# Fewer score groups, an earlier weight load and a narrower spread in a decoder layer

## The chip, the core and the metric

The kernel runs on one core of one Trainium2 chip. TensorE (PE) does the matrix products, VectorE (DVE) and ScalarE (ACT) the elementwise work and the moves out of the accumulators (PSUM), GpSimd (POOL) a few small things, and SyncE (SP) issues nearly all transfers. The metric is the device time of one execution, in microseconds (us).

## The reference

One layer of a decoder trunk, 512 tokens of width 1024, in float32:

```
mod = silu(c) @ w_ada + b_ada            # six rows of 1024: shift, scale, gate, twice
h = rmsnorm(x) * (1 + scale1) + shift1
q,k,v (sliding), q,k,v (differential), two gates = split(h @ w_in)
A: 8 heads of 64, 2 key heads, window 128, ALiBi, a learned sink in the softmax
B: 4 heads, two causal softmax maps each, p0 - lambda * p1, times v; per-head rmsnorm
x += gate1 * ((sigmoid(ga) * (A @ w_a) + sigmoid(gd) * (B @ w_b)) @ w_out)
x += gate2 * convffn(rmsnorm(x) * (1 + scale2) + shift2)
out = rmsnorm(x)
```

## The kernel before

Products are taken at nearly full float32 precision from a faster float type: each operand is split into a high and a low part, and `mm3` (L119 to L121) issues three matmuls, high x high, high x low, low x high. The weights come as float32 into one of four buffers with the tag "raw" (512 KB each); `split` then makes the high half on ACT (a cast, L115) and the low half on DVE (a subtraction, L116). A raw buffer is free once both have read it. All these loads are issued by SP, in one order, and SP waits where the next load's buffer is not yet free.

The work has four stages. To about 60 us: two modulation rows, the first norm, and the first six column blocks of the input projection. From 60 to about 330 us: the attention with the rest of the projection, the gates and the branch products. Then the output projection, the MLP (up L1126, down L1735), and a short tail.

In the attention the order of PE's program is written out by hand (`tc.manual_schedule` for the tensor engine); DVE, ACT, POOL and SP get theirs from the framework's scheduler, which places instructions by its own estimates, by priorities (`tc.high_priority`) and by marks that an instruction comes behind another (`tc.issue_after`). PE's filler is `fill(n)`: n steps, each one `mm3` of 128x512 matmuls of the current projection unit. Units lie in the list `units`; two are loaded ahead. `after(n, fn)` puts a small piece of work behind n further steps, and every eighth step the generator `ada_rows` is advanced by one.

Between filler stand the attention's own pieces:

- Sliding heads, in four pairs (i = 0 to 3). `swa_scores` (L532) computes the scores of two query blocks as a group of small matmuls on the upper and lower 64 rows of the array side by side (`mm3_rows`, L126), into two PSUM banks; a DVE reduction (L559) adds the bias and takes the row maximum. `swa_softmax`: ten exponentials on ACT (L571, L574), then DVE divides (L578 to L582). `swa_transpose` (L593): transposes on PE, copies to `pT` on ACT (L595). `swa_values` (L604): the product with v in two column tiles of 64 columns; `evac` (L430, L431) takes the result out as high part on ACT and low part on DVE (`outal`).
- Differential heads, 16 steps of (head, query block). `diff_scores` (reduction at L673), `diff_softmax` (exponentials L687, scalings L692 and L693 on DVE), `diff_transpose` (L702), and once a head `diff_values` (`od`).

PSUM tags: two banks for filler, three for scores (`sbank`), two for transposes and small spreads (`tbank`), one for the value products (`vbank`).

The other modulation rows are made in the attention by `ada_rows`: for each of four rows and two halves, four loads `ra` of two k-blocks (L750), each followed in the same step by two DVE multiply-adds into `arow` (L755, L757). The 128 partitions of `arow` are then summed: `split` makes `arh` and `arl`, and `ada_spread` multiplies them by a square of ones on PE (L766, L767, tile `pr`), copies one row out on ACT (L769) and sends it to memory on POOL's queue (`mod_rows`, L770).

The order of the sliding pieces in one turn of the loop is:

```
        if more:
            swa_scores(i + 1, 0)
        fill(SWA_FILL[3])
        swa_transpose(i, 0)
        fill(SWA_FILL[4])
        swa_transpose(i, 1)
        if more:
            swa_scores(i + 1, 2)
        fill(SWA_FILL[5])
        ...
        nxt = {0: (), 1: (s + 1,), 2: (s + 1,), 3: (s + 1, s + 2)}[n] if s < 15 else ()
```

The last line is the differential loop's choice of the blocks that are scored in a step.

Of the kernel before, what the change touches and what calls it, by code (L numbers as in the profile page):

```python
# [8 lines left out]
F32 = mybir.dt.float32  # L9
# [44 lines left out]
def kernel(  # L54
# [41 lines left out]
    def sbank(name, shape=(P, S)):  # L96
        return bank("s", 3, list(shape), name)
# [7 lines left out]
    def raw_tile(shape, name):  # L105
        return wp.tile(shape, F32, tag="raw", bufs=4, name=name)
# [26 lines left out]
    warm = cpool.tile([P, 1], F32, name="warm")  # L133
    nc.vector.memset(warm, 0.0)
    nc.scalar.activation(warm, warm, AF.Exp)
    onesr = cpool.tile([P, P], F32R, name="onesr")
    nc.vector.tensor_copy(onesr, ones)
    mhalf = cpool.tile([P, 4], F32, name="mhalf")
    nc.gpsimd.memset(mhalf, -0.5)
    qsc = cpool.tile([P, 4], F32, name="qsc")  # L140
# [388 lines left out]
    class Pair:  # L529
        pass  # L530

    def swa_scores(i, n0):  # L532
        if n0 == 0:
            c = pairs[i] = Pair()
            c.mx, c.nm, c.lsum, c.es = (
                ap.tile([P, 2, NT], F32, tag=t, bufs=2, name=f"{t}{i}") for t in ("mx", "nm", "lsum", "es")
            )
            c.sb = [ap.tile([P, 2, P], F32, tag="st0", bufs=2, name=f"st{i}_0")]
            c.sb += [ap.tile([P, 2, 256], F32, tag="st", bufs=ST, name=f"st{i}_{n}") for n in range(1, NT)]
            c.pT = []  # L540
        c = pairs[i]
        sps = [sbank(f"sw{i}_{n0}_{j}", (P, 2, 256)) for j in range(2)]
        for n in (n0, n0 + 1):
            w = P if n == 0 else 2 * P
            k0 = max(0, n - 1) * P
            qs, ks = slice(n * P, (n + 1) * P), slice(k0, k0 + w)
            mm3_rows([
                (
                    sps[j][:, n - n0, :w],
                    [qa[64 * j : 64 * j + 64, i, b, qs] for b in range(2)],  # L550
                    [ka[64 * j : 64 * j + 64, b, ks] for b in range(2)],
                )
                for j in range(2)
            ])
        for n in (n0, n0 + 1):
            w = P if n == 0 else 2 * P
            for j in range(2):
                with tc.high_priority(offset=HP):
                    c.last = nc.vector.tensor_tensor_reduce(  # L559
                        c.sb[n][:, j, :w], sps[j][:, n - n0, :w], dsw[:, 256 - w : 256], 1.0, -3e38, ALU.add, ALU.max,  # L560
                        c.mx[:, j, n : n + 1],
                    )

# [20 lines left out]
    def swa_transpose(i, j):  # L584
        c = pairs[i]
        pt = ap.tile([P, 1024], F32, tag="aTh" if j == 0 else "aTl", bufs=2, name=f"pT{i}_{j}")
        for b in range(2):
            wb = 512 if b == 0 else 384
            tp = tbank(f"tp{i}_{j}_{b}")
            for m in range(wb // P):  # L590
                kb, n = 2 * b + m // 2, 2 * b + m // 2 + m % 2
                off = (kb - max(0, n - 1)) * P
                nc.tensor.transpose(tp[:, m * P : (m + 1) * P], c.sb[n][:, j, off : off + P], ident)  # L593
            with tc.high_priority(offset=HP):
                nc.scalar.copy(pt[:, b * 512 : b * 512 + wb], tp[:, :wb])  # L595
        c.pT.append(pt)

    def swa_values(i):
        o = vbank(f"oa{i}")
        for kb in (0, 2, 1, 3):  # L600
            w = P if kb == 3 else 2 * P
            for j in range(2):
                rows = slice(64 * j, 64 * j + 64)
                nc.tensor.matmul(  # L604
                    o[rows, kb * P : kb * P + w], va[:, kb, rows],
                    pairs[i].pT[j][:, kb * 256 : kb * 256 + w],
                    start=kb == 0, stop=kb == 3, tile_position=(0, 64 * j),
                )
        evac(outa[0][:, i], outa[1][:, i], o)


    heads = {}
# [35 lines left out]
    def diff_scores(*ss):  # L648
        ops = []
        for s in ss:  # L650
            h, n = divmod(s, NT)
            t = heads[h]
            w = (n + 1) * P
            if n == 0:
                firsts[h] = [sbank(f"sd{h}_{m}", (P, 2, 256)) for m in range(2)]
            sps = [firsts[h][m][:, n, :w] if n < 2 else sbank(f"sd{h}_{n}_{m}")[:, :w] for m in range(2)]
            mm3_rows([
                (
                    sps[m],
                    [t[64 * m : 64 * m + 64, b, n * P : (n + 1) * P] for b in range(2)],  # L660
                    [t[64 * m : 64 * m + 64, 2 + b, :w] for b in range(2)],
                )
                for m in range(2)
            ])
            ops.append((s, sps, w))
        for s, sps, w in ops:
            h, n = divmod(s, NT)
            mx = ap.tile([P, 2], F32, tag="dmx", bufs=3, name=f"dmx{h}_{n}")
            pm = []
            for m in range(2):  # L670
                st = ap.tile([P, w], F32, tag="st", bufs=ST, name=f"sd{h}_{n}_{m}")
                with tc.high_priority(offset=HP):
                    nc.vector.tensor_tensor_reduce(  # L673
                        st, sps[m], ddf[:, 512 - w : 512], 1.0, -3e38, ALU.add, ALU.max, mx[:, m : m + 1]
                    )
                pm.append(st)
            scored[s] = mx, pm
# [62 lines left out]

    mod_rows = tc.dram_tile([4, D], F32, name="mod_rows")

    def ada_rows():
        for idx in range(4):
            for hf in range(2):
                c0 = (2 + idx) * D + hf * S
                ac = big.tile([P, S], F32, tag="sq2", name=f"arow{idx}{hf}")
                for k in range(0, KT, 2):
                    r = raw_tile([P, 2, S], f"ra{idx}{hf}_{k}")
                    nc.sync.dma_start(r, wada[k * P : (k + 2) * P, c0 : c0 + S].rearrange("(a p) n -> p a n", p=P))  # L750
                    with tc.high_priority(offset=HP // 2) if tick[0] > ADA_EASY else ExitStack():
                        for a in range(2):
                            cc = cs[:, k + a : k + a + 1]
                            if k + a == 0:
                                nc.vector.tensor_scalar_mul(ac, r[:, a], cc)  # L755
                            else:
                                nc.vector.scalar_tensor_tensor(ac, r[:, a], cc, ac, ALU.mult, ALU.add)  # L757
                    yield
                ah = big.tile([P, S], F32R, tag="g2b0", name=f"arh{idx}{hf}")
                al = big.tile([P, S], F32R, tag="g2b1", name=f"arl{idx}{hf}")  # L760
                split(ah, al, ac)
                after(ADA_LAG, lambda idx=idx, hf=hf, ac=ac, ah=ah, al=al: ada_spread(idx, hf, ac, ah, al))

    def ada_spread(idx, hf, ac, ah, al):
        pr = tbank(f"pr{idx}{hf}")
        nc.tensor.matmul(pr, onesr, ah, start=True, stop=False)  # L766
        nc.tensor.matmul(pr, onesr, al, start=False, stop=True)  # L767
        row = ac[0:1, :]
        nc.scalar.copy(row, pr[0:1, :])  # L769
        nc.gpsimd.dma_start(mod_rows[idx : idx + 1, hf * S : (hf + 1) * S], row)  # L770


    pair_w = {}
# [29 lines left out]
    add_head(0)  # L803
    add_head(1)
    fill(SWA_FILL[0])
    swa_scores(0, 0)
    with tc.issue_after(pairs[0].last.ins):
        fill(SWA_FILL[1])
        swa_scores(0, 2)
    with tc.issue_after(pairs[0].last.ins):  # L810
        swa_softmax(0)
        fill(1)
# [2 lines left out]
        fill(SWA_FILL[2] - 1)  # L815
    for i in range(SWA_PAIRS):
        more = i + 1 < SWA_PAIRS
        if more:
            swa_scores(i + 1, 0)
        fill(SWA_FILL[3])  # L820
        swa_transpose(i, 0)
        fill(SWA_FILL[4])
        swa_transpose(i, 1)
        if more:
            swa_scores(i + 1, 2)
        fill(SWA_FILL[5])
        if more:
            swa_softmax(i + 1)
        fill(SWA_FILL[6])
        swa_values(i)  # L830
        fill(SWA_FILL[7])
# [11 lines left out]
    for s in range(4 * DIFF_HEADS):  # L843
        h, n = divmod(s, NT)
        if n == 0 and 0 < h < 3:
            add_head(h + 1)
        elif s == 12:
            add_gate_a(2)
            add_gate_a(3)
        fill(DIFF_FILL[1])  # L850
        nxt = {0: (), 1: (s + 1,), 2: (s + 1,), 3: (s + 1, s + 2)}[n] if s < 15 else ()
        if nxt:
            diff_scores(*nxt)
        fill(DIFF_FILL[2])
        diff_transpose(s)
        for z in nxt:
            diff_softmax(z)
        if n == 0 and h:
            diff_values(h - 1)
            fill(DIFF_FILL[3])  # L860
# [926 lines left out]
```

## Time and profile before

| | us |
|---|---|
| runs shown | 706.75, 707.45, 707.52; median 707.45 |
| the profiled execution | 708.24, of which the span from first to last instruction is 705.4 |
| TensorE clock granted, mean | 0.994 |
| ACT busy in the span | 383.9 |
| DVE busy from 120 to 220 us | 83.03 of 100 |
| modulation multiply-adds (L757), 56 of them | 41.9, 747 ns each |
| modulation loads `ra`, 32 of 512 KB | 4.2 median from issue to landing |

A line of the costliest groups names the line of code, the engine, the operation, what it writes and reads (by the program's names, buffer numbers left out), partitions x elements, and the count; then the busy time and the mean of one in ns; then the idle time of the engine just before these instructions with what ended it. The records of filler matmuls overlap, so that one takes 0.39 us although the next starts 0.23 later: what PE can do is read from start to start. Busy times of an engine that is not the one that sets the end cost nothing by themselves.

### The profile page before, as it was taken

How to read it: one execution, taken by the hardware profiler on the slowest of the kernel's cores; microseconds unless marked ns; L12 is line 12 of the kernel's file. 1: busy time of each engine (PE TensorE's matmuls, PEld its weight loads, DVE VectorE, ACT ScalarE, POOL GpSimd, SP SyncE). 2: the span in 40 equal slices, each digit the busy share in tenths (PEclk: the TensorE clock that was granted, in tenths of full speed). 3: DMA queues.
4: the chain of work that ended last, by engine and by line, in shares of the span. 5: the costliest groups of instructions: out<-in, count | busy, mean ns of one | idle time of the engine just before them, and what ended most of it. 6: DMA issues, size and time to landing. Idle time of an engine off the chain costs nothing. (4 is left out here: it accounts for less than half of the span.)

```text
span 705.4 us, 11197 instructions
## 1 busy us (share of the span) xinstructions
PE 685.0 (97%) x4155; PEld 597.1 (85%) x4155; DVE 578.4 (82%) x1107; ACT 383.9 (54%) x676; POOL 82.2 (12%) x100
## 2 busy tenths in 40 slices
PE   6999999999999999999999999999999999999994
PEld 6777777777787888888889999999999999888884
DVE  5998968788985766773579899888888999979996
ACT  3646766545543333431468656555555666656664
POOL 3000000000011000000030111111101102530300
PEclk9999999999999999999999999999999999999998
DMA  9983624263543774529617888786979748996803
GB/s 311 302 262 98 201 61 154 67 199 90 170 153 100 262 214 142 186 93 288 187 33 148 197 199 204 177 209 182 208 204 230 164 143 204 197 200 191 158 0 119
DMA packets 115861, 121.80 MB, mean 173 GB/s; under 512 B 4415, under 2 KB 93280, under 8 KB 115808
## 3 DMA queue, kind: packets, MB, share of 16 engines
q1 hardware_dynamic: 96894, 95.09, 42.7%
q0 software_dynamic: 18720, 25.73, 21.6%
q8 instruction: 32, 0.52, 0.3%
q10 hardware_dynamic: 194, 0.28, 0.1%
q14 instruction: 21, 0.17, 0.1%
HBM read 118.97 MB, written 2.11 MB: 172 GB/s over the span
## 5 line engine op out<-in xcount | busy, mean ns | idle before, releaser
L1126 PE MATMUL up<-t,m_whi 128*128 128x256 f32 x528 | 96.1, 283 | 0.0
L1126 PEld LDWEIGHTS up<-t,m_whi 128*128 128x128 f32 x528 | 82.3, 192 | 0.0
L1126 PE MATMUL up<-t,m_wlo 128*128 128x256 f32 x264 | 74.7, 283 | 0.1
L1126 PE MATMUL up<-bh,p_wlo 128*128 128x256 f32 x232 | 65.7, 284 | 0.7 <-DVE p_wlo L1069 0.7
L1126 PE MATMUL up<-bh,p_whi 128*128 128x256 f32 x232 | 65.6, 283 | 0.0
L1126 PE MATMUL up<-bl,p_whi 128*128 128x256 f32 x232 | 65.6, 283 | 0.0
L1126 PEld LDWEIGHTS up<-t,m_wlo 128*128 128x128 f32 x264 | 50.6, 192 | 0.3 <-DVE m_wlo L1069 0.3
L1126 PEld LDWEIGHTS up<-bh,p_wlo 128*128 128x128 f32 x232 | 44.5, 192 | 1.1 <-DVE p_wlo L1069 1.1
L1126 PEld LDWEIGHTS up<-bh,p_whi 128*128 128x128 f32 x232 | 44.5, 192 | 0.0
L1126 PEld LDWEIGHTS up<-bl,p_whi 128*128 128x128 f32 x232 | 44.5, 192 | 0.0
L757 DVE SCALAR_TENSOR_TENSOR arow<-ra,cs,arow 128x512 f32<-128x512 f32 x56 | 41.9, 747 | 2.6 <-DMA ra<-in_w_ada_dram 1.8
L1037 POOL DMA_DIRECT2D s<-in_w_up_dram x21 | 27.0, 1361 | 142.9 <-DMA s<-in_w_up_dram 78.0
L1069 DVE TENSOR_TENSOR m_wlo<-s,m_whi 128x1024 fp32r<-128x1024 f32 x31 | 37.7, 1217 | 2.0 <-ACT m_whi L1065 2.0
L1065 ACT CAST m_whi<-s 128x1024 fp32r<-128x1024 f32 x31 | 32.5, 1047 | 9.4 <-DVE s L1059 5.9
L1126 PE MATMUL up<-t,p_whi 128*128 128x256 f32 x176 | 32.2, 283 | 0.0
L687 ACT ACTIVATE sd<-sd,dmx 128x128 f32<-128x128 f32 (+3 forms) x32 | 17.8, 556 | 23.2 <-DVE dmx L685 15.9
L175 POOL TENSOR_TENSOR r<-ms,mhalf 128x1 f32<-128x1 f32 (+1 forms) x16 | 13.2, 828 | 144.7 <-DVE ms L173 74.0
L1126 PEld LDWEIGHTS up<-t,p_whi 128*128 128x128 f32 x176 | 27.4, 192 | 0.2 <-issue 0.2
L1133 ACT ACTIVATE gT<-a,cv 128x512 f32<-128x512 f32 x22 | 17.7, 813 | 17.6 <-DVE a L1168 17.3
L770 POOL DMA_DIRECT2D mod_rows<-arow x8 | 4.3, 540 | 193.7 <-ACT arow L769 193.5
L1065 ACT CAST p_whi<-wa 128x1024 fp32r<-128x1024 f32 x18 | 18.7, 1041 | 12.0 <-PE up L1126 7.2
L1126 PE MATMUL up<-t,p_wlo 128*128 128x256 f32 x88 | 24.9, 283 | 0.0
(478 smaller groups left out, 2073.0 us busy)
## 6 DMA issues: line engine op xcount, KB each, us to landing
ra<-in_w_ada_dram SPq DMA_DIRECT2D x32, 512.0 KB, 4.2
wa<-in_w_up_dram SPq DMA_DIRECT2D x22, 512.0 KB, 4.6
s<-in_w_up_dram SPq DMA_DIRECT2D x21, 512.0 KB, 5.1
s<-in_w_up_dram POOLq DMA_DIRECT2D x21, 512.0 KB, 7.0
adaw<-in_w_ada_dram SPq DMA_DIRECT2D x16, 512.0 KB, 4.9
w<-in_w_in_dram SPq DMA_DIRECT2D x12, 512.0 KB, 4.1
a<-in_w_up_dram SPq DMA_DIRECT2D x11, 512.0 KB, 4.8
b<-in_w_down_dram SPq DMA_DIRECT2D x10, 512.0 KB, 4.7
```

Of the source, the lines that this page charges most:

```text
L175: nc.gpsimd.tensor_tensor(r0, ms, mhalf[:, :n], ALU.pow)
L687: nc.scalar.activation(pm[m], pm[m], AF.Exp, bias=mx[:, m : m + 1], scale=slope, accum_out=lsum[:, m : m + 1])
L757: nc.vector.scalar_tensor_tensor(ac, r[:, a], cc, ac, ALU.mult, ALU.add)
L770: nc.gpsimd.dma_start(mod_rows[idx : idx + 1, hf * S : (hf + 1) * S], row)
L1037: nc.gpsimd.dma_start(dst, upblock(*blk), accum_op=ALU.add)
L1065: nc.scalar.copy(W[J, name][0], R[J, SRC[name]])
L1069: nc.vector.tensor_sub(lo, R[J, SRC[name]], hi.bitcast(F32))
L1126: nc.tensor.matmul(o[u], w[:, k, cu], b[:, k], start=name in ("p1", "m5", "p2") and k == 0 and x == 0, stop=k == 3 and x == 2, skip_group_ ...
L1133: nc.scalar.activation(grow(j), av[J][:, u], AF.Identity, bias=cv[:, 66 + j : 67 + j], scale=cv[:, 44 + j : 45 + j])
```

## The change

- The scores of all four blocks of sliding pairs 1 to 3 are computed as one group, which now stands behind the first filler of the turn; pair 0 keeps two groups. The fourth bank comes from `vbank`, which the value products use as well. In the differential part blocks 0 and 1 of a head are scored together, as before, and blocks 2 and 3 together, with one of the four banks from `vbank`. From 20 groups 13 are left.
- `ada_rows` issues each load one step (eight filler steps) ahead of its use. `arow` alternates between two buffers. There is no split into high and low parts: `ada_spread` takes the float32 row as it is, in four matmuls of 128 columns whose outputs lie in four column tiles of 32 columns; ACT copies the whole 128x128 result to a buffer of its own, and four rows of it are sent to memory.
- The exponentials of pair i+1 are placed behind the last copy to `pT` of pair i, and the copies of the value products get high priority.

```
-    onesr = cpool.tile([P, P], F32R, name="onesr")
-    nc.vector.tensor_copy(onesr, ones)
...
-    def swa_scores(i, n0):
+    def swa_scores(i, blocks):
...
-        sps = [sbank(f"sw{i}_{n0}_{j}", (P, 2, 256)) for j in range(2)]
-        for n in (n0, n0 + 1):
+        sps = {
+            (g, j): vbank(f"sw{i}_{g}_{j}").rearrange("p (a q) -> p a q", a=2)
+            if len(blocks) == NT and (g, j) == (1, 1) else sbank(f"sw{i}_{g}_{j}", (P, 2, 256))
+            for g in sorted({n // 2 for n in blocks}) for j in range(2)
+        }
+        for n in blocks:
...
-                nc.scalar.copy(pt[:, b * 512 : b * 512 + wb], tp[:, :wb])
+                c.copied = nc.scalar.copy(pt[:, b * 512 : b * 512 + wb], tp[:, :wb])
...
-        evac(outa[0][:, i], outa[1][:, i], o)
+        with tc.high_priority(offset=HP):
+            evac(outa[0][:, i], outa[1][:, i], o)
...
-            sps = [firsts[h][m][:, n, :w] if n < 2 else sbank(f"sd{h}_{n}_{m}")[:, :w] for m in range(2)]
+            sps = [
+                firsts[h][m][:, n, :w] if n < 2 else (vbank if n + m == 4 else sbank)(f"sd{h}_{n}_{m}")[:, :w]
+                for m in range(2)
+            ]
...
+    def ada_load(idx, hf, k):
+        c0 = (2 + idx) * D + hf * S
+        r = raw_tile([P, 2, S], f"ra{idx}{hf}_{k}")
+        nc.sync.dma_start(r, wada[k * P : (k + 2) * P, c0 : c0 + S].rearrange("(a p) n -> p a n", p=P))
+        return r
...
+        todo = [(idx, hf, k) for idx in range(4) for hf in range(2) for k in range(0, KT, 2)]
+        r = ada_load(*todo[0])
+        yield
+        for (idx, hf, k), job in zip(todo, todo[1:] + [None]):
+            nxt = ada_load(*job) if job else None
+            if k == 0:
+                ac = big.tile([P, S], F32, tag=("sq2", "g2b1")[hf], name=f"arow{idx}{hf}")
...
+            if k == KT - 2:
+                after(ADA_LAG, lambda idx=idx, hf=hf, ac=ac: ada_spread(idx, hf, ac))
+            r = nxt
+            yield
...
-        pr = tbank(f"pr{idx}{hf}")
-        nc.tensor.matmul(pr, onesr, ah, start=True, stop=False)
-        nc.tensor.matmul(pr, onesr, al, start=False, stop=True)
-        row = ac[0:1, :]
-        nc.scalar.copy(row, pr[0:1, :])
-        nc.gpsimd.dma_start(mod_rows[idx : idx + 1, hf * S : (hf + 1) * S], row)
+        pr = tbank(f"pr{idx}{hf}", (P, P))
+        for g in range(4):
+            gs = slice(32 * g, 32 * g + 32)
+            nc.tensor.matmul(
+                pr[gs], ones[:, gs], ac[:, g * P : (g + 1) * P], start=True, stop=True, tile_position=(0, 32 * g)
+            )
+        row = big.tile([P, P], F32, tag="g2b0", name=f"row{idx}{hf}")
+        nc.scalar.copy(row, pr)
+        nc.gpsimd.dma_start(
+            mod_rows[idx, hf * S : (hf + 1) * S].rearrange("(g n) -> g n", g=4), row[0:P:32]
+        )
...
+        fill(SWA_FILL[3])
         if more:
-            swa_scores(i + 1, 0)
-        fill(SWA_FILL[3])
+            swa_scores(i + 1, range(NT))
         swa_transpose(i, 0)
         fill(SWA_FILL[4])
         swa_transpose(i, 1)
-        if more:
-            swa_scores(i + 1, 2)
         fill(SWA_FILL[5])
         if more:
-            swa_softmax(i + 1)
+            with tc.issue_after(pairs[i].copied.ins):
+                swa_softmax(i + 1)
...
-        nxt = {0: (), 1: (s + 1,), 2: (s + 1,), 3: (s + 1, s + 2)}[n] if s < 15 else ()
+        nxt = (s + 1, s + 2) if n % 2 and s < 15 else ()
```

## The prediction

> **What bounds the kernel now.** I read the page's head and busy shares first, then the table by stretches of time, then who waits for whom in the attention (60 to 340 us), then single stretches of the timeline. The page:
>
> ```profile
> span 705.4 us, 11197 instructions
> PE 685.0 (97%) x4155; PEld 597.1 (85%) x4155; DVE 578.4 (82%) x1107; ACT 383.9 (54%) x676; POOL 82.2 (12%) x100
> ```
>
> The table by stretches (busy us and count of each engine, clock, DMA share, GB/s):
>
> ```profile
> 120.00:220.00 100.00, 97.89 (x517) 77.28 (x516) 83.03 (x226) 53.03 (x122) 5.89 (x6) 1.00 0.47 140
> 220.00:340.00 120.00, 120.00 (x537) 98.93 (x537) 76.09 (x98) 38.97 (x51) 7.05 (x11) 1.00 0.60 187
> ```
>
> PE is the bound: in 60 to 340 it stands for 2.1 us, all between 120 and 220. What it executes sets the time, and what holds it now is small. The waits of PE there (total, times, longest):
>
> ```profile
> PE td L702 <- DVE sd L693: 1.6, 3, 1.1
> PE od L120 <- DVE aTl L431: 0.5, 1, 0.5
> ```
>
> **Part 1, scores in 13 groups instead of 20.** A score group is a visit to matmuls with 64-row tiles amid 128x512 filler. One such visit on PE's timeline:
>
> ```profile
> 125.74 0.40 PE L121 MATMUL pA<-outah,wba_l 128*128 128x512 f32 x1
> 126.07 0.79 PE L126 MATMUL sd<-qkv 64*128 64x384 f32 x6
> 126.79 0.50 PE L119 MATMUL pA<-outah,wba_h 128*128 128x512 f32 x1
> 127.13 0.39 PE L120 MATMUL pA<-outal,wba_h 128*128 128x512 f32 x1
> ```
>
> From 125.74 to 127.13 are 1.39 us; two filler slots of 0.23 are in it, so the group costs 0.93. Its six matmuls run in three pairs, each pair's two row tiles start 4 ns apart and the pairs 0.17 apart: 0.52 of streaming. The remaining 0.41 is paid on entering and leaving (0.33 instead of 0.23 before the group, the same after the first filler behind it). The sliding group at 82.14 gives the same: 1.54 less 0.46 is 1.08, streaming six pairs of 0.11, overhead 0.41. Merging drops seven visits (three sliding, four differential; the matmuls stay): 7 x 0.41 = 2.9 us less, bounds 2.5 to 3.3 (sliding blocks 2 and 3 stood behind transposes, where I find 1.10 by difference). This lies on the path, as PE has no slack.
>
> **Part 2, the spread of a modulation row.** Before, two full-array matmuls:
>
> ```profile
> 163.64 0.39 PE L121 MATMUL pw<-hThB,w_l 128*128 128x512 f32 x1
> 163.87 0.39 PE L766 MATMUL pr<-arh,onesr 128*128 128x512 f32 x1
> 164.10 0.40 PE L767 MATMUL pr<-arl,onesr 128*128 128x512 f32 x1
> ```
>
> 0.48 us each, no switch. After: four fp32 matmuls of 128x128 in 32-column tiles. No row has four column tiles; the nearest is the value product, with two:
>
> ```profile
> 114.83 0.40 PE L121 MATMUL pw<-hThB,w_l 128*128 128x512 f32 x1
> 115.15 1.73 PE L604 MATMUL oa<-pT,va 128*64 128x256 f32 x16
> ```
>
> Its entry is 0.32 too; its two tiles start 6 ns apart, an fp32 matmul is two records (104 ns per 128 columns, 208 per 256), and a whole group costs 1.87, of which 1.46 streams: overhead 0.41 again. So with four tiles side by side: 0.21 + 0.41 = 0.62, +0.14 each, eight times **+1.1**. Ends: one after another, 0.83 + 0.41 = 1.25, +0.77 each, +6.2; no switching cost, 0.21 to 0.3, -0.2 each, -1.6. I take 1.1, as both tile kinds seen run side by side and both pay 0.41. The Trainium skill, "TensorEngine Tiling (Array Packing)", Key Properties, says that changing the tiling mode, unlike changing the tile, drains TensorE. It speaks against this part: by the streaming alone the eight spreads would save 8 x 0.27 = 2.2 and the whole sum be -4.8; by the rule they pay a visit each and it is the -1.5 below. The 0.41 on row tiles and on two column tiles agrees with the rule.
>
> The row copy (128x128 for 1x512) and the DMA (4 rows for 1) are one instruction each as before, off the path.
>
> Gone are eight casts on ACT (0.62 each) and eight subtractions 128x512 on DVE (0.60 to 0.69): 5 us on each, neither the bound; nothing on the path. The ones tile is one small copy at the start. Gone too is DVE's wait before a new row for the old row's DMA:
>
> ```profile
> DVE arow L755 <- DMA mod_rows<-arow: 5.7, 4, 3.4
> DVE arow L757 <- DMA ra<-in_w_ada_dram: 1.8, 3, 0.8
> ```
>
> PE's stalls do not stand behind those four, so I credit only what follows in part 4.
>
> **Part 3, loads a step ahead.** SP issues loads in order, and each waits for one of four raw slots. In the issue order of the changed program the loads stand as before among the weights, but each use on DVE has moved forward by up to 80 places, while its load still waits for a slot that DVE itself frees: ra01_0 for w768_1's low half, ra01_4 for w1792_1's, ra10_4 for wga1's, ra10_6 for the use of ra10_4. Such a load lands 3.7 to 4.4 us after its issue (page, 4.2). Laying the new DVE order out with the old durations (low half 1.13, multiply-add 0.66, four scalings 1.0), DVE reaches the use some 2 us before the data: 2.3 at ra01_0, 2.0 at ra01_4, 2.8 at ra10_4, 2.0 at ra10_6, under 1 elsewhere. The 1.8 above becomes about 10. Behind the waiting instruction are softmax scalings and, twice, the subtraction outal that frees the values bank.
>
> That bank is new on the path: pairs 1 to 3 put their fourth score bank there. Between values(i) and scores(i+2) lie five filler steps, 3.5 us. The release takes a copy and a subtraction (0.56 + 0.68), the waiting multiply-add (0.7) and the rest of a 2 us wait: PE loses some 0.35 at each of pairs 2 and 3, **+0.7**, between 0 (load lands as early as DVE comes) and 2.6 (the whole wait falls behind the values). In the differential part the bank is freed by two ACT reads (0.60, 0.68) which ended 1.5 us ahead of the next scores (148.3 against 149.85); nothing there.
>
> The exponentials of a pair (4.1 us on ACT) move ahead of the weight cast (1.04). They have the filler and the values ahead of the next transposes as cover; the cast then is later by up to 4.1, its weights are loaded two units (over 10 us) ahead. I take 0; without the cover it would be 1.0 a pair, 3 us.
>
> **Part 4, the old stalls.** With blocks 2 and 3 scored together, block 3's probabilities are made one block earlier; the stalls before its transposes (0.17 at 164.7, 0.33 at 213.3) go. The one of 1.14 at 144.96 had this on DVE ahead of it:
>
> ```profile
> 141.84 0.74 DVE L757 SCALAR_TENSOR_TENSOR arow<-ra,cs,arow 128x512 f32<-128x512 f32 x1
> 143.28 0.74 DVE L757 SCALAR_TENSOR_TENSOR arow<-ra,cs,arow 128x512 f32<-128x512 f32 x1
> 144.47 0.74 DVE L693 SCALAR_TENSOR_TENSOR sd<-sd,dls,sd 128x128 f32<-128x128 f32 x2
> ```
>
> In the new order both multiply-adds stand elsewhere and a low half (1.13) stands beside the exponentials: 0.2 remains. The 0.5 of od at the end stays, one filler step against a copy and a subtraction. Late next is block 2's transpose: from its scores to it were 9.5 to 9.8 us in the four heads; without the separate block-3 visit and with its streaming 0.69 there are 9.4. The chain now: 0.8 to 1.5 until DVE takes the scores, four reductions 2.2 (two before), four exponentials 2.6, scalings 1.5, together 7.1 to 7.8; 1.6 to 2.3 are left for a cast (1.04) or a load's wait (2). I take 0.25 a head, 1.0, between 0 and 4. Stalls: 0.2 + 0.5 + 1.0 = 1.7 for 2.1, **-0.4**, between -1.6 and +2.6.
>
> **Sum.** -2.9 + 1.1 + 0.7 - 0.4 = -1.5 us. The profiled execution took 708.24 (span 705.4 and 2.84 around it); it becomes 706.7. It stood 0.79 above the median of the runs shown (707.45), so I predict **705.9**.
>
> **The rivals.**
> - Everything reaches the path. The banks come in time, all old stalls go (2.1) and the spreads cost 0.05 each: -2.9 - 2.1 + 0.4 = -4.6, 702.9. For it: DVE loses 5 us of work and the 5.7 of waits. Against it: the loads' slots, and od's 0.5 has no reason to go.
> - Slower: held loads. DVE stands at the multiply-adds for the whole load, behind it the values bank (1.3 at each of two pairs) and block 2's probabilities (1.0 in each of four heads). -2.9 + 1.1 + 2.6 + (0.2 + 0.5 + 4.0 - 2.1) = +3.4, 710.9. It decides as soon as PE's stalls in the attention exceed 2.1 + 2.9 - 1.1 = 3.9 us. For it: the order of slots and uses. Against it: much of such a wait falls into time in which DVE idles anyway (83 of 100 us busy).
> - Column tiles one after another: -2.9 + 6.2 + 0.3 = +3.6, 711.1. Against it: the 6 ns of two tiles. The Trainium skill, "TensorE: Matmul & The Clock Gate", Part 3, has tiles of 32 columns running together, starts some 4 ns apart; no run here shows four.
> - It does nothing: new stalls of 3 to 4 us eat the merges, 707.4.
>
> **How the numbers follow.** Forecast 0.5 (705 to 707), all reaches the path 0.15, held loads 0.22, serial tiles 0.06, nothing 0.07. Within 0.2% (1.4 us; about what runs of this kernel can tell from no change) is 706.0 to 708.9. Of the forecast's half, 0.35 lie below it, 0.13 in it, 0.02 above: faster 0.35 + 0.15 = 0.50; same 0.13 + 0.07 = 0.20; slower 0.02 + 0.22 + 0.06 = 0.30. Range: 702.8 to 710.7, which leaves out the slower half of the held loads, most of the serial tiles, and a little below; the likeliest case alone has 704.5 to 707.3.
>
> **What would show it.** Score visits: 13, each merged one about 0.41 under the sum of its parts; another price fells part 1. Spread: start to start from the filler before to the filler after 0.62 more than the fillers' slots; four starts within some 15 ns, or 0.2 apart if serial. DVE waits for ra: about 10 us in all, and rows of PE waiting at sw L126 for outal and at td for sd; if they are above 4 us the forecast fails to the slow side, if below 1 to the fast one. From 220 on nothing should differ but the shift and the spreads.

## The result and the profile after

The changed kernel takes 705.53 us (median of 10 runs, 704.81 to 707.48) against 707.42 for the kernel before (10 runs beside them). The ratio is 0.9977, with a 95% interval of 0.9968 to 0.9986: 1.0 to 2.3 us faster. The forecast was 705.9. The page of the profiled execution, head and busy shares:

```profile
span 702.9 us, 11248 instructions
PE 681.7 (97%) x4203; PEld 592.6 (84%) x4203; DVE 571.2 (81%) x1098; ACT 376.3 (54%) x668; POOL 82.4 (12%) x100
```

PE is the bound as before. The table by stretches (busy us and count of each engine, granted clock, DMA share, GB/s):

```profile
120.00:220.00 100.00, 98.73 (x546) 78.31 (x546) 79.39 (x216) 48.86 (x118) 5.70 (x6) 1.00 0.43 129
220.00:340.00 120.00, 120.00 (x559) 97.84 (x558) 71.34 (x90) 37.23 (x49) 7.41 (x11) 1.00 0.58 180
340.00:360.00 20.00, 20.00 (x93) 16.45 (x92) 13.12 (x24) 9.01 (x19) 1.51 (x2) 1.00 0.32 104
```

PE stands 1.3 us between 120 and 220 where it stood 2.1, but 0.8 between 60 and 120, where it stood not at all: from 60 to 340 it stands 2.1 us in both. It stands not at all between 340 and 360, where the kernel before had 0.65 at a transpose (its line of the groups):

```profile
L1221 PE MATMUL th<-ident,xn 128*128 128x128 f32 x2 | 0.6, 300 | 0.7 <-DVE xn L1211 0.7
```

What the changed kernel's PE waits for between 60 and 340 (total, times, longest):

```profile
PE od L120 <- DVE aTl L429: 0.9, 1, 0.9
PE pk L119 <- ACT vT L635: 0.5, 1, 0.5
PE tp L595 <- ACT row L785: 0.3, 1, 0.3
PE od L119 <- ACT aTh L428: 0.3, 1, 0.3
```

The three waits of td are gone from the list; the waits for the ACT copies vT and row are new, and the one before the last values product (od, two lines) has grown from 0.5 to 1.1. A merged score group on PE's timeline:

```profile
125.91 0.40 PE L121 MATMUL pA<-outah,wba_l 128*128 128x512 f32 x1
126.24 1.50 PE L126 MATMUL sd<-qkv 64*128 64x384 f32 x12
127.67 0.50 PE L119 MATMUL pA<-outah,wba_h 128*128 128x512 f32 x1
128.00 0.39 PE L120 MATMUL pA<-outal,wba_h 128*128 128x512 f32 x1
```

From 125.91 to 128.00 are 2.09; less two filler slots it is 1.64, where two groups cost 0.93 and 1.10. The new spread:

```profile
133.98 0.39 PE L121 MATMUL pga<-hThB,wga_l 128*128 128x512 f32 x1
134.30 0.43 PE L781 MATMUL pr<-arow,ones 128*32 128x128 f32 x8
134.66 0.50 PE L119 MATMUL pA<-outah,wba_h 128*128 128x512 f32 x1
134.99 0.39 PE L120 MATMUL pA<-outal,wba_h 128*128 128x512 f32 x1
```

1.01 less 0.45 is 0.56, for 0.48 before: eight records (two for each of four tiles) in 0.36 from the group's first start to the next filler. The four tiles' first records start 6 to 7 ns apart, where the prediction had cited some 4, so the tiles run side by side. And DVE's waits for the modulation loads between 60 and 340, which were 1.8 us:

```profile
DVE arow L770 <- DMA ra<-in_w_ada_dram: 20.2, 16, 4.1
DVE arow L768 <- DMA ra<-in_w_ada_dram: 5.5, 3, 2.3
```

By stages (from the first instruction): the first scores come 0.24 earlier (61.24 for 61.48; the first 20 us were granted a clock of 1.00, 0.91 before). From there to the first output-projection matmul it is 255.70 for 257.26, **1.56 less**. From there to the first up matmul 0.71 less, with the wait of 0.65 gone. After that 340.4 in both.

### The profile page after: what moved, and what is told of

Its sections match the earlier page's. It is cut to its first block, busy times and chain, and to the rows that moved or that the text cites. A ratio compares the mean times of both kernels' runs of the same rounds, so it can differ in the third digit from the quotient of the medians.

```text
span 702.9 us, 11248 instructions
## 1 busy us (share of the span) xinstructions
PE 681.7 (97%) x4203; PEld 592.6 (84%) x4203; DVE 571.2 (81%) x1098; ACT 376.3 (54%) x668; POOL 82.4 (12%) x100
## 5 line engine op out<-in xcount | busy, mean ns | idle before, releaser
L786 POOL DMA_DIRECT2D mod_rows<-row x8 | 4.9, 614 | 206.3 <-ACT row L785 206.3
```

Of the source, the lines that this page charges most:

```text
L786: nc.gpsimd.dma_start(mod_rows[idx, hf * S : (hf + 1) * S].rearrange("(g n) -> g n", g=4), row[0:P:32])
```

## The experiments

My theory was the prediction's: PE's own work sets the time, a visit to row tiles costs some 0.4 us, and DVE's long waits for loads are hidden. The rivals: that DVE's relief by the new rows brings the gain and the merges little; and that the loads' waits cost part of it. The last run below was made before the two ahead of it; where their expectations speak of the run that moved copies, they mean that one. Ratios are to the kernel before on the same chip, 0.9977 being that of the change.

**The merged scores alone**, on the kernel before (its `swa_scores`, its loops and the bank list as in the change):

```
+            swa_scores(i + 1, range(NT))
...
+        nxt = (s + 1, s + 2) if n % 2 and s < 15 else ()
```

> The kernel before with the merged scores alone (13 groups, the values bank shared); rows, loads and exponentials as before. My theory, that the visits to row tiles are what is saved: seven visits of 0.41 us less, and the stalls before block 3's transposes (0.5 in sum) gone, new stalls at the values bank and block 2 up to 1: 2.5 to 3.2 below the kernel before, 704.3 to 704.9; a merged pair of groups costs 1.62 on PE where two cost 2.03. Rival, that the merges are hidden and the gain of the whole comes from DVE's relief by the new rows: 707.0 to 707.8.

Measured 716.03, ratio 1.0125 (1.0110 to 1.0139): 9 us slower, outside both. PE's new waits in the profiled execution, which was the longest of the four at 719.05:

```profile
PE td L709 <- DVE sd L700: 5.4, 2, 2.9
PE sw L126 <- DVE outal L431: 2.2, 1, 2.2
PE pv L641 <- ACT pT L599: 1.1, 1, 1.1
```

The merges need the rest of the change. The waits are for differential probabilities, for the values bank, and for a transposes' bank. In all PE stands 10.6 us from 60 to 340, 2.1 before, and behind three of these waits the granted clock drops to half for some microseconds (last section).

**The new rows alone**, on the kernel before (its `ada_rows` and `ada_spread` replaced by the change's):

```
-    def ada_rows():
+    def ada_load(idx, hf, k):
...
+    def ada_rows():
```

> The kernel before with the new rows alone (loads one step ahead, no split, four column tiles in the spread). My theory: eight spreads dearer by 0.08 each (0.56 for 0.48), +0.6, DVE's waits for loads (over 20 us in sum) mostly hidden, old stalls moved by half a us either way: 707.4 to 708.6, not faster. Rival, DVE's relief: the stalls of 1.14 and 0.65 go and the time falls to 705.5 to 706.2.

Measured 709.40, ratio 1.0035 (1.0023 to 1.0047): slower by 2.5, worse than the theory's upper end, and the relief rival falls. PE waits for td 2.7 us (1.6 before) and pays the dearer spreads. That accounts for 1.7 of the 2.5; the profiled execution took 708.06, near the lowest of the seven, and where the rest goes is open. This run is without the mark and the priority too, so it tells of the rows alone, not of the change without the merges.

**The exponentials and the values' copies as before**, the rest of the change kept:

```
-            with tc.issue_after(pairs[i].copied.ins):
-                swa_softmax(i + 1)
+            swa_softmax(i + 1)
...
-        with tc.high_priority(offset=HP):
-            evac(outa[0][:, i], outa[1][:, i], o)
+        evac(outa[0][:, i], outa[1][:, i], o)
```

> The changed kernel with the exponentials and the copies of the values placed as before. My theory: the wait of 0.54 of a filler matmul for the copy vT, which stands behind the exponentials, goes, and nothing else is held up, since the transposes have filler ahead of them: 704.8 to 705.5. Rival, that the earlier exponentials are needed for the merged scores: transposes of pairs 1 to 3 then wait 0.5 to 1 each for the scaled probabilities, 706.5 to 708.

Measured 709.96, ratio 1.0053 (1.0035 to 1.0070): 5.4 us above the changed kernel. I had taken the place of the exponentials as worth nothing and had not priced the priority; without the two the change is a loss. The waits are 3.0 at pair 2's scores for outal and 1.8 at pv for a copy pT, not the scaled probabilities that the rival named. The next two runs part them.

**The priority kept, the exponentials as before** (only the first hunk above):

> The changed kernel with the exponentials of a pair placed as before, but the values' copies still with high priority (on DVE the subtraction outal then stays ahead of the next pair's reductions). Theory now, that two parts of the third change carry separate stalls, the bank's and the transposes' banks': the wait of 3.0 at pair 2's scores stays away, the 1.8 of the transposes pv for a copy pT that stands behind exponentials comes, the 0.54 goes: 706.5 to 707.3. Rival, that the priority alone does it: 705.0 to 705.6.

Measured 710.82, ratio 1.0050 (1.0038 to 1.0063). The wait at pv is 3.4, that at the scores 0.6. ACT's timeline shows why:

```profile
104.81 0.30 ACT L573 ACTIVATE es<-nm,sink 128x4 f32<-128x4 f32 x1 [4.32 <-DVE nm L572]
105.01 0.39 ACT L576 ACTIVATE st<-st,nm 128x128 f32<-128x128 f32 x1
105.40 0.94 ACT L597 COPY pT<-tp 128x512 f32<-128x512 f32 x2
```

Two exponentials of pair 3 stand ahead of pair 2's copies and wait 4.3 us for their maximum; the copies would free the bank that pv needs. With the mark `issue_after(copied)` the exponentials cannot stand there.

**The exponentials moved, no priority** (only the second hunk):

> The changed kernel without the high priority of the values' copies; the exponentials stay where the change put them. On DVE the subtraction outal of pair 0 then stands behind reductions of pair 2 whose scores need the bank that it frees. Theory: PE waits about 3.0 at pair 2's scores and nothing else changes: 708.0 to 709.0. Rival, that the exponentials' place alone does it: 705.3 to 706.0.

Measured 711.94, ratio 1.0070 (1.0054 to 1.0085). The wait is the one expected, but 5.4 us and not 3.0, in a profiled execution of 714.68, the longest of the six; and a new one of 2.1 stands at the transposes th of the output projection. On DVE, among others:

```profile
87.44 0.28 DVE L561 CUSTOM_DVE_ANT_0 st<-sw,dsw 128x128 f32<-128x128 f32 x1
88.55 0.68 DVE L429 TENSOR_TENSOR outal<-oa,outah 128x512 fp32r<-128x512 f32 x1
90.85 0.42 DVE L561 CUSTOM_DVE_ANT_0 st<-sw,dsw 128x256 f32<-128x256 f32 x1 [1.62 <-PE sw L126]
```

The subtraction that frees the bank stands behind the first reductions of the very scores that need it, and these behind a load's wait and a low half. The third line then waits for PE, which waited for the second. Either line alone costs as much as the two together (6.6 and 5.2 us for 5.4): their prices do not add up.

**The old rows in the changed kernel** (the reverse of the second experiment, with the `onesr` tile):

> The changed kernel with the rows as before: load in the step of the use, split into high and low parts, two 128x512 matmuls. If the rows' part only costs PE eight times 0.08 and its waits are hidden: 704.3 to 705.3. If the old rows' place on DVE is what made block 2's transposes wait 2.5 and 2.9 in the run with the merged scores alone, so that merges pay only with the new rows: 709 to 712.

Measured 712.20, ratio 1.0069 (1.0046 to 1.0092): the second theory. PE waits 5.5 us for differential probabilities (td), twice. On DVE, ahead of the first and the second:

```profile
138.18 0.49 DVE L763 TENSOR_SCALAR arow<-ra,cs 128x512 f32<-128x512 f32 x1 [3.02 <-DMA mod_rows<-arow]
161.08 1.21 DVE L116 TENSOR_TENSOR w_l<-w,w_h 128x1024 fp32r<-128x1024 f32 x1
162.21 0.61 DVE L701 SCALAR_TENSOR_TENSOR sd<-sd,dls,sd 128x384 f32<-128x384 f32 x1
```

A new row waits 3.0 for the old row's transfer right ahead of the reductions of head 1's first scores; and a low half stands between the scalings of its block 2. So the merges do not pay without the new rows, and the new rows alone did not pay either. The change without the merges was not run: that the rows pay only with them is not shown. Which half of the rows does it, the next two ask.

**The loads in the step of the use**, the rest of the change kept:

```
-        for (idx, hf, k), job in zip(todo, todo[1:] + [None]):
-            nxt = ada_load(*job) if job else None
+        for idx, hf, k in todo:
+            r = ada_load(idx, hf, k)
```

> The changed kernel with each load of modulation weights issued in the step of its use, as before; two row buffers, no split and four column tiles stay. If the step ahead is what keeps block 2's and block 0's transposes from waiting: waits of 2 to 5 us in the differential part as with the old rows, 708 to 711. If the second row buffer and the dropped split do it, and the step ahead nothing: 705.0 to 706.5.

Measured 708.86, ratio 1.0022 (1.0007 to 1.0038): between the two, 3.2 above the changed kernel, with runs from 705.7 to 711.6. Its waits:

```profile
PE tp L595 <- DVE qkv L429: 2.3, 1, 2.3
PE td L708 <- DVE sd L699: 1.9, 1, 1.9
```

The first is a load's wait of 1.8 on DVE, which held the subtraction behind it that frees a transposes' bank.

**The old spread, loads a step ahead** (split, one row buffer, two 128x512 matmuls):

```
+                split(ah, al, ac)
+                after(ADA_LAG, lambda idx=idx, hf=hf, ac=ac, ah=ah, al=al: ada_spread(idx, hf, ac, ah, al))
```

> The changed kernel with the old spread: split into high and low parts, two 128x512 matmuls, one row buffer, the row copied into it; the loads stay one step ahead. PE executes 0.6 less (0.48 for 0.56, eight times). If the step ahead is what matters: 704.5 to 705.5. If the row buffer, whose reuse waits for the old row's transfer, and the eight subtractions matter: 2 to 5 us of waits at td, 707.5 to 711.

Measured 713.43, ratio 1.0073 (1.0051 to 1.0096): the row buffer and the split, which this run does not part. PE waits 5.5 for td in the same two places as with the old rows (2.70 and 2.85), though it executes less. So the new spread, dearer on PE, goes with a row buffer and without a split, and these free DVE; the step ahead is worth some 3 us beside it, and nothing that shows beside the old spread (ratios 1.0069 and 1.0073).

**No modulation loads**:

```
-        r = ada_load(*todo[0])
+        r = None
...
+                            nc.vector.tensor_scalar_mul(ac, hTh[k + a].bitcast(F32), cc)
```

> The changed kernel without the 32 loads of modulation weights in the attention; the multiply-adds read the normed input, which is long there, so the four modulation rows are wrong. DVE's 25.7 us of waits for these loads are gone, and so is their use of raw buffers. My theory, that these waits are hidden: at most the stalls behind them go (0.26 at pair 2's scores, some of the 1.1 at the last values), 704.5 to 705.5. Rival, that they cost PE its gain: 703.0 to 704.0.

Measured 716.42, ratio 1.0137 (1.0124 to 1.0150): confounded. With nothing to wait for, the scheduler put multiply-adds into the first stage, where PE then waited 7.8 for DVE (`pa` for `ac`), and the first scores came at 73.0 instead of 61.2. From the first scores to the end it took 641.75, the changed kernel 641.67. That agrees with the waits being hidden there, but the order on DVE is another too, so it is no proof.

**A later last values product**:

```
-    fill(1)
+    fill(4)
     diff_values(DIFF_HEADS - 1)
```

> The changed kernel with the last values product four filler steps later instead of one, nothing else. Theory: its 1.13 of waiting goes and is not given back before the output projection's norm: 0.8 to 1.1 below the changed kernel, 704.3 to 704.9. Rival, that a later stage waits the more (0.8 at the transposes th of the output projection, as in the run that moved copies too): 705.3 to 705.8.

Measured 704.97, ratio 0.9966 (0.9952 to 0.9980). The 1.13 is gone, and 1.2 us appear at the transposes th of the output projection: in the profiled execution (705.54) all of it is given back, as the rival said. The median lies 0.6 under the changed kernel's, and the interval holds both answers.

**The same with the copy vT first on ACT**:

```
-            nc.scalar.copy(vT, o)
+            with tc.high_priority(offset=2 * HP):
+                nc.scalar.copy(vT, o)
```

> As the one before, with the copy vT at the highest priority on ACT: its wait of 0.54 goes. Theory: 0.5 less than that run, 703.8 to 704.4. Rival, that the values' copies move behind it and PE waits as much at the next pair's scores (0.62 in the run that moved both copies): no difference.

Measured 704.06, ratio 0.9954 (0.9941 to 0.9967): inside the theory's range and the lowest of all. It lies 0.9 under the run before it, but the two intervals overlap, so the step from there is not told from noise. Against the changed kernel it is about 1.6 less, and its interval ends just below where that one's begins. Its waits from 60 to 375:

```profile
PE th L1239 <- DVE xn L1229: 0.9, 1, 0.9
PE tp L595 <- ACT row L786: 0.6, 1, 0.6
PE td L709 <- DVE sd L700: 0.6, 1, 0.6
PE th L1239 <- ACT braw L1249: 0.2, 1, 0.2
```

**That with the copy row first as well**:

```
-        nc.scalar.copy(row, pr)
+        with tc.high_priority(offset=2 * HP):
+            nc.scalar.copy(row, pr)
```

> The changed kernel with the last values product four filler steps later instead of one, and the copies vT and row with the highest priority on ACT. Theory: the waits of 1.13 at the last values, 0.54 for vT and 0.26 for row were on PE's path and nothing else stands behind them: 1.5 to 1.9 below the changed kernel, 703.0 to 704.2 on the scale of these runs. Rival, that the products behind the last values become late in turn: 705 to 706.

Measured 704.61, ratio 0.9962 (0.9948 to 0.9975): not told from the run without it. The wait for row is 0.6 with and without, so a priority did not move it; 0.6 at pair 3's scores (outal) came instead of vT's.

## Why the prediction was right, point by point

The total was right, and nearest where it was worked out: the attention, -1.5 forecast, -1.56 in the profile. Inside it errors cancel: the four parts are off by 0.4, -0.6, 0.9 and -0.7, so that the sum agrees to 0.1 is luck, while the mechanism of parts 1 and 2 (PE's own work sets the time) held, with PE standing 2.1 us in both. I cost a group from the start of the filler ahead of it to that of the second behind it, less two slots.

- **Part 1, -2.9: -2.5.** The sliding turns save 0.44, 0.44 and 0.43 (the middle one before its new wait), as worked out. The heads save 0.40, 0.28, 0.22 and 0.28: in the last three, block 3's group had stood directly behind the small matmuls `pss` and shared its entry with them. The visit's price holds only amid filler. One reading was loose: in the group at 126.07 only the second and third pair start 0.17 apart, the first and second 0.28; that tenth is part of the 0.41, which stands. The 2.5 is read from starts on PE at the places of the merges, not from a run without them.
- **Part 2, +1.1: +0.5.** Side by side, as taken, but 0.56 and not 0.62 (0.35 over the streaming, not 0.41), and no dearer than before where the spread abuts other small matmuls. The drain that the Trainium skill states ("TensorEngine Tiling (Array Packing)", Key Properties) fits the row: 0.32 until the first start, as ahead of row tiles.
- **Part 3, +0.7: +1.6.** The values bank cost 0.26 at pair 2 and nothing at pair 3. The step that failed is "I take 0" for the exponentials: it named the weight cast as the work behind them, and the one that hurt was the copy vT, which frees a filler bank (0.70 from start to start at 95.7). And "off the path" for the row copy: it stood behind a cast of 1.06 and held a transposes' bank (0.61 at 110.7). The loads' waits were seen at their places (1.9, 1.3, 1.5 and 1.6 for 2.3, 2.0, 2.8 and 2.0), but in all they were 26 us and not 10, 16 of it from 217 us on, where no PE work stands close behind.
- **Part 4, -0.4: -1.1 by difference.** It is what is left of the 1.56; at the places named the stalls come to 1.3 (0.13 and 1.13) for 2.1, which is -0.9. Block 2 never waited (1.0 taken), head 1's first transpose waits 0.13 (0.2), the last values 1.13 (0.5).
- **Outside the sum**: 0.65 at the output projection's transposes, gone, and 0.24 ahead of the attention. In the medians of ten runs the gain is 1.9.

The two rows of part 3, the first filler of a unit that waited for vT's bank, and the row copy:

```profile
95.73 0.50 PE L119 MATMUL pk<-hThA,w_h 128*128 128x512 f32 x1 [0.54 <-ACT vT L635]
110.41 0.27 ACT L785 COPY row<-pr 128x128 f32<-128x128 f32 x1
```

What the prediction had not seen is how the parts hang together. It did not name the priority, priced the exponentials' place at nothing and the new rows at a small loss; taken away singly, the priority, the mark and the new rows cost 6.6, 5.2 and 6.5 us. The "held loads" rival named the right places, the values bank and the differential probabilities. By these runs, that it did not come true is the doing of those parts.

## What to carry to other kernels

When a group grows by borrowing a bank, find the instruction that frees the bank in its engine's order, and see that it stands ahead of whatever waits for the group: here that one place was worth 6 us, more than the merges. An in-order queue is judged by what stands behind each wait: of 26 us of waits for loads on DVE, the one place where PE is seen to pay is 0.26 at pair 2's scores, while one wait of 4 us in front of a copy on ACT cost PE 3.4. Take a change apart before calling a part of it harmless: here the merges alone and the rows alone made the kernel slower, and neither the rows nor the mark nor the priority could be left out. The mark and the priority alone, and the change without the merges, were not run.

## What the hardware showed that I had not expected

A wait of PE has a tail. In the executions above, PE's granted clock falls to 0.50 in or after many waits of over 2 us and stays there for 3.4 or 6.8 us. The wait of 5.4 us without the priority, in the table by stretches of 1 us (PE busy, PEld, DVE, ACT, POOL, clock, DMA share, GB/s):

```profile
89.00:90.00 1.00, 0.62 (x6) 0.66 (x8) 0.23 (x1) 0.00 (x0) 0.00 (x0) 0.50 1.07 297
91.00:92.00 1.00, 1.00 (x5) 1.00 (x6) 1.00 (x7) 0.00 (x0) 0.00 (x0) 0.50 0.94 250
93.00:94.00 1.00, 1.00 (x4) 0.81 (x3) 0.00 (x0) 0.19 (x1) 0.00 (x0) 0.56 0.08 24
94.00:95.00 1.00, 1.00 (x8) 0.83 (x8) 0.00 (x0) 0.49 (x1) 0.00 (x0) 1.00 0.00 0
```

Work resumes at 89.4 and runs at half clock until about 93.9, its filler matmuls 0.43 apart instead of 0.23: 4.5 us in which about half is lost, some 2 more. The same follows waits of 2.25, 2.52 and 2.88 with the merged scores alone, 2.98 and 3.4 in the two runs with the exponentials as before, 2.6 and 2.8 with the old rows, and the 2.1 at th without the priority; it did not follow 2.70 and 2.85 in the profiled execution with the old spread, nor 2.32 and 1.94 with the loads in the step of their use.

The traces' clock records tell these apart. Within an execution the clock changes only at multiples of 3.41 us from one another. Laid out on that grid, from 60 to 375 us, every cell of 3.41 us in which PE stood 2.05 us or more is followed by a half clock, and no cell with 1.91 or less was followed by a fall. The four waits without a tail each lie across an edge of the grid, with at most 1.91 in one cell; those of 2.52 and 2.88 have 2.05 and 2.28 in one. Idle time is not the whole measure, though: ahead of 60 us, in the run without modulation loads, cells with 1.4 and 1.5 were followed by a half clock too, and with the old rows the clock stayed at 0.50 for a second cell, from 167.6 to 171.0, after one without idle time. So whether a wait costs more than itself depends on where it falls on the grid, and that differs from execution to execution.

This fits the spread of the kernel with the old spread: its five longest executions, 714.2 to 715.0, had a mean granted clock of 0.983 to 0.987, its four shortest, 708.1 to 710.7, one of 0.992 to 0.995. It does not explain the spread with the loads in the step of their use, 705.7 to 711.6 at 0.990 to 0.997 without order; that cause is open. The Trainium skill ("TensorE: Matmul & The Clock Gate", Part 1) tells of such a gate, with a free-running window of some 3.4 us; the steps of 3.41 agree, and waits down to 2.1 set it off here. So a wait of 2.5 us cost about 4 where the half clock followed it, and the changed kernel, whose longest single wait in the attention is 0.9, pays no tail.
